# A decoder step's input product: seven products for eight in four more quads, another order of groups, recurrence tables per pair

## The chip, the core and the metric

The kernel runs on one core of a Trainium2 chip. The metric is the device time of one execution in microseconds (us); less is better.

## The reference

One layer of a hybrid decoder over 2048 prompt tokens and 64 sample tokens (8 sequences of 8), 2112 in all, in float32. The parts that matter here:

```python
xn = rms_norm(x, norm_pre)                               # (tokens, 1024)
z = jnp.einsum('btd,de->bte', xn, w_in)                  # w_in 1024 x 4096
v_pool, g_pool, u_lru, g_lru = ...                       # four times 1024 columns of z
y_pool, new_pool = pool_mixer(v_pool, pool_buf, ...)     # sliding means of 2, 4, 8, 16 tokens
                                                         # by channel group, then a 256x256 map
xs, new_conv = causal_conv(u_lru, conv_buf, ...)         # width 4, per channel
y_lru, new_h = rg_lru(xs, h0, ...)                       # two gates by 128x128 matmuls per head,
                                                         # then h = a*h + u along the tokens
mixed = jnp.concatenate([y_pool * silu(g_pool), y_lru * silu(g_lru)], -1)
out = jnp.einsum('bte,ed->btd', mixed, w_out)            # w_out 2048 x 1024
return x + rms_norm(out, norm_post), new_pool, new_conv, new_h
```

The pool and LRU mixers carry state along the tokens, so the tokens go through in order.

## The kernel before

**Tiling.** The tokens are cut into three thirds m = 0, 1, 2 of 704 (two column halves of 352 each, `CW`). In each third the product with `w_in` is done in 16 *quads* (m, p, kind): the kind is V (pool input), G (pool gate), U (LRU input) or L (LRU gate), and p = 0..3 is a group of 256 channels. A quad is a 2 x 2 block problem: two halves of the 1024 inputs, two blocks of 128 channels, two halves of the tokens. Names carry all three: `wG2_...` is a weight tile of G of group 2 in the first third, `w1G2_5` the one for product 5 of the same quad in the second.

**Products.** Every float32 operand is split into a high part (ACT casts it to fp32r, `x_hi` and `hi_lo`) and the rest (DVE subtracts, `x_lo`); a product adds hi·hi, hi·lo and lo·hi, so one product of 512 inputs is 4 x 3 = 12 matmuls of 128 x 352 (`quad_product`). In the first third a quad takes 8 plain products (`plain_slot`). In the second and third thirds it takes 7 products of sums of blocks, in the manner of Strassen and Winograd (`quad_slot`), numbered 1, 5, 6, 3, 2, 7, 4. They build up in three PSUM tiles: `a` takes 1, 6, 7, 4 in turn, `e` takes 5, 3, and `d` takes 2; after each, ACT copies the tile out (`put_copy`) or DVE adds it to what was copied (`put_sum`), and PE may not write the tile again before that. The x operands X11, T1, T2, X22, T3, X21, T4 are blocks of x and sums of blocks, in an SBUF tile XN; the `transition` between two thirds makes them. The weight operands are sums of blocks of `w_in`, made on DVE from four raw tiles (`s_sums`), split, used, and stored to a DRAM tile `wsd` from which later thirds load them. A quad of the second third that finds no stored sums and makes its own from raw tiles is a *late* quad (`is_late`). For V and G of groups 1, 2 and 3 the sums are made during the first third, with nothing to use them there (`s_early`), so ten of the second third's 16 quads are late.

**After the product.** V quads feed the pool chain (scan, differences, a map by 128 x 128 matmuls, names `y`, `dh`, `dl`, `pw`), U quads the convolution and the gate matmuls (`r`, `i`, `xh`, `xl`, `lw`), L and G quads SiLU gates. The LRU recurrence runs per head in `lru_chain`: tanh, square root, arctan and two sines on ACT, which need three sets of ACT tables, then a scan on DVE. Results go to DRAM (`mixed`). Last comes the product with `w_out`.

**What sets the order.** A planner in the kernel's own code writes the program out. `one_slot` issues one product, then `run_jobs` lets waiting jobs (generators that ask for an engine, a wait or a DMA) fill ACT, DVE and GpSimd to the end of that slot by estimated costs; a job's rank adds a small penalty. Each engine then runs its instructions in exactly this order. Weight tiles turn over in `W_BUFS = 7` buffers and are asked for `AHEAD = 6` slots before use; raw tiles have eight buffers, two quads' worth. All loads of weights and x go out in order from the one queue of SP. In the first third groups come 0, 1, 2, 3, and so in the others.

```python
key = {1: "a", 6: "a", 7: "a", 4: "a", 5: "e", 3: "e", 2: "d"}[pid]
...
if not first:
    pe_after(t["f" + key])      # not before the tile's last copy or sum
...
W_BUFS = 7
```

At the second transition the first blocks of `w_out` (`wb11_0` to `wb11_4`) are loaded and cast too (`region_chain`), into the space of the tile XA that held the raw x.

Of the kernel before, what the change touches and what calls it, by code (L numbers as in the profile page):

```python
# [16 lines left out]
P = 128  # L17
# [43 lines left out]
AHEAD = 6  # L61
TABLE_COST = 1.4
# [5 lines left out]
X_LEAD = (5, 5)  # L68
# [7 lines left out]
def hymba_kernel(  # L76
# [24 lines left out]
    def t_done(n):  # L101
        t_live[0] -= n
# [107 lines left out]
    XA = sb.tile([P, 4 * QW], F32, tag="XA", bufs=1, name="XA")  # L210
# [18 lines left out]
    def q_raw(name):  # L229
        if name in "AB":  # L230
            i = "AB".index(name)
            return XA[:, 2 * QW * i:2 * QW * (i + 1)]
        return XN[:, BASE[name]:BASE[name] + 2 * QW].bitcast(F32)
# [3 lines left out]

    def q3(name, i):
        b = BASE[name] + i * QW
        return XN[:, b:b + QW].rearrange("p (k t) -> p k t", t=CW)  # L240

    def xq(name, k, i):
        b = BASE[name] + i * QW + k * CW
        return XN[:, b:b + CW]
# [126 lines left out]
    def region(r, k, i):  # L371
        p = (r * KT + k) * 2 + i
        if p >= 10:
            p -= 10
            return XN[:, PIECE * p:PIECE * (p + 1)]
        if not x2_box:
            x2_box.append(sb.tile([P, 4 * QW], F32R, tag="XA", bufs=1, name="XA2"))
        return x2_box[0][:, PIECE * p:PIECE * (p + 1)]
# [83 lines left out]
    def product_short(bank, a, r):  # L462
        for k in range(KT):
            ah = a[k // 4][:, (k % 4) * P:(k % 4 + 1) * P]
# [45 lines left out]
    def short_a(q):  # L510
# [3 lines left out]
        for e in range(2):  # L514
            t = t_tile(f"as{q}_{e}", F32R)[:, :PIECE] if e else x2_box[0][:, 10 * PIECE:11 * PIECE]
            ts.append(t)
# [3 lines left out]
            h3 = t.rearrange("p (b t) -> p b t", t=P)  # L520
            split(h3[:, :, :n], h3[:, :, n:2 * n], r, nc.scalar, nc.vector)
# [200 lines left out]
    for m_ in range(NM):  # L722
        for p_ in range(NG):
            L_ = [(m_, p_ - 1, "L")] if p_ else []
            if m_ == LM and p_ == NG - 1:
                QUADS += [(m_, p_, "V")] + L_ + [(m_, p_, "U"), (m_, p_, "G")]
            elif (m_, p_) == (0, 1):
                QUADS += L_ + [(m_, p_, "V"), (m_, p_, "G"), (m_, p_, "U")]
            else:
                QUADS += [(m_, p_, "V"), (m_, p_, "G")] + L_ + [(m_, p_, "U")]  # L730
        QUADS.append((m_, NG - 1, "L"))
# [19 lines left out]
    def spawn(gen, ready=None, rank=2, then=()):  # L751
        job = {"gen": gen, "ready": T[0] if ready is None else ready, "rank": rank, "then": list(then)}
# [30 lines left out]
    def run_jobs(end):  # L783
        moved = True
        while moved:
# [14 lines left out]
            for job in jobs:  # L800
# [3 lines left out]
                req = job["req"]  # L804
                late = s + (TABLE_COST if len(req) > 2 and table[0] not in TABLES[req[2]] else 0.0)
                late += PENALTY[job["rank"]]
# [20 lines left out]
    IDLE = [XN[:, BASE[n] + 1024 * i:BASE[n] + 1024 * (i + 1)] for n in ("X11", "T2", "T1") for i in range(2)]  # L827
    S_OF = {5: "22", 6: "11", 7: "21", 3: "12"}
    n_idle = [0]
# [35 lines left out]
    def plain_tile(q, n):  # L865
        t = w_tiles[q, n] = half_tile(f"w{q[2]}{q[1]}_{n}")
        store = (flat_of(t), q[2], q[1], PLAIN_PID[n]) if n in PLAIN_PID else None
        w_jobs[q, n] = spawn(hi_lo(t[:, 0, :], t[:, 1, :], w_rawt[q, n], store, (q, n)), rank=0)
# [20 lines left out]
    def s_early(q):  # L889
        def made(i):  # L890
            n = n_idle[0] % len(IDLE)
            b = IDLE[n]
            n_idle[0] += 1
            if n in places:
                force(places[n], True)
            places[n] = spawn(hi_lo(b[:, :512], b[:, 512:], w_rawt[q, S_OF[S_PID[i]]], (b, q[2], q[1], S_PID[i])),
                              clock["V"] + HOP, rank=1)
            early.append(places[n])
        early.append(spawn(s_sums(q, made), rank=1))

    early, places = [], {}
# [1062 lines left out]
```

## Time and profile before

| | before |
|---|---|
| median of 3 runs | 1156.71 us (1156.38 to 1162.74) |
| profiled execution | 1159.3 us |
| its span, first to last instruction | 1157.6 us |
| mean granted TensorE clock | 0.995 |
| PE busy | 1127.9 us (97%) |
| DVE busy | 826.7 us (71%) |
| ACT busy | 656.0 us (57%), 88.5 of it in 69 table loads |
| GpSimd (POOL) busy | 160.4 us (14%) |
| DMA | 322.10 MB, mean 278 GB/s |

PE is TensorE's matmuls, DVE is VectorE, ACT is ScalarE, SP the engine that issues most DMAs. Names such as L323 are lines of the kernel. In waits, "A <- B" says that A's engine stood idle until B's was done. A granted clock under 1.00 means that PE ran slower than full speed. The second third's first product starts at 296 us, the third third's at 551, the output product at 815.

### The profile page before, as it was taken

The page shows a single profiled execution, that of the slowest core. Times are in us where ns is not written, and L with a number is a line of the kernel's source. Part 1 is how long each engine was busy: PE and PEld are TensorE (multiplying, and loading weights), DVE is VectorE, ACT ScalarE, POOL GpSimd, SP SyncE. Part 2 cuts the span into 40 slices and gives each one's busy share as a digit, 9 for nine tenths or more (in the row PEclk, how much of TensorE's full clock was granted, in tenths as well). Part 3 has the DMA queues.
Part 4 walks back from the last instruction along what each step waited for, and adds up shares of the span by engine and source line. Part 5 has one row for each costly group of instructions (what it writes and reads, how often), then busy time and mean ns, then how long its engine had stood idle before and what let it go on. Part 6 is the DMA issues. An engine that isn't in the chain of part 4 may idle for free. (4 is left out here: it accounts for less than half of the span.)

```text
span 1157.6 us, 17742 instructions
## 1 busy us (share of the span) xinstructions
PE 1127.9 (97%) x6274; PEld 1056.3 (91%) x6274; DVE 826.7 (71%) x1323; ACT 656.0 (57%) x1112; POOL 160.4 (14%) x264
## 2 busy tenths in 40 slices
PE   7999999999999999999899999999999999999996
PEld 6999999999999999989899999999888888888885
DVE  6796783859768667578857674746567678778777
ACT  5376658777577847567464846374755233344232
POOL 4200100002001010101111111101000003211232
PEclk9999999999999999999999999999999999999999
DMA  9656877895897889996989999998679677776563
GB/s 329 233 195 234 306 279 272 325 352 185 292 342 271 317 319 326 382 387 225 370 280 380 397 351 370 358 353 292 207 202 291 182 207 221 207 233 185 164 182 127
DMA packets 177464, 322.10 MB, mean 278 GB/s; under 512 B 24736, under 2 KB 86432, under 8 KB 177376
## 3 DMA queue, kind: packets, MB, share of 16 engines
q1 hardware_dynamic: 173536, 303.67, 76.3%
q0 software_dynamic: 3840, 17.30, 3.8%
q8 instruction: 49, 0.80, 0.3%
q14 instruction: 39, 0.32, 0.1%
HBM read 218.51 MB, written 102.15 MB: 277 GB/s over the span
## 5 line engine op out<-in xcount | busy, mean ns | idle before, releaser
L151 ACT ACT_TABLE_LOAD x69 | 88.5, 1283 | 1.9 <-PEq L1943 0.8
L458 PE MATMUL p<-XN,s 128*128 128x512 f32 (+1 forms) x224 | 86.8, 387 | 0.0
L459 PE MATMUL p<-XN,s 128*128 128x512 f32 (+1 forms) x224 | 86.8, 387 | 0.0
L460 PE MATMUL p<-XN,s 128*128 128x512 f32 (+1 forms) x224 | 86.7, 387 | 0.0
L1217 DVE SCALAR_TENSOR_TENSOR xs<-u,parT,xs 128x704 f32<-128x704 f32 (+1 forms) x72 | 67.8, 956 | 16.1 <-ACT xs L1206 15.9
L451 POOL TENSOR_TENSOR xr<-ac,xr 128x512 f32<-128x512 f32 x27 | 48.5, 1815 | 207.1 <-DVE ac L592 97.7
L1180 DVE SCALAR_TENSOR_TENSOR g<-y,parT,g 128x352 f32<-128x352 f32 x48 | 27.9, 582 | 53.9 <-PE y L253 53.2
L253 PE MATMUL zL<-XN,wL 128*128 128x352 f32 x384 | 65.0, 325 | 0.6 <-DVE wL L323 0.6
L253 PEld LDWEIGHTS zL<-XN,wL 128*128 128x128 f32 x384 | 62.7, 188 | 0.9 <-DVE wL L323 0.9
L140 ACT CAST s<-a 128x512 fp32r<-128x512 f32 x48 | 28.7, 616 | 57.8 <-DVE a L451 44.9
L571 ACT ACTIVATE p<-ac 128x512 f32<-128x512 f32 (+1 forms) x32 | 18.8, 587 | 75.1 <-DVE ac L451 75.1
L451 DVE TENSOR_TENSOR a<-a,a 128x512 f32<-128x512 f32 x48 | 33.0, 690 | 29.7 <-DMA a<-mixed 25.6
L458 PE MATMUL p<-XN,a 128*128 128x512 f32 x137 | 54.2, 396 | 0.0
L460 PE MATMUL p<-XN,a 128*128 128x512 f32 x137 | 54.2, 396 | 0.0
L459 PE MATMUL p<-XN,a 128*128 128x512 f32 x137 | 54.2, 395 | 0.0
L253 PE MATMUL y<-dh,pw 128*128 128x352 f32 x192 | 54.1, 323 | 0.0
L460 PEld LDWEIGHTS p<-XN,s 128*128 128x128 f32 x224 | 42.1, 188 | 9.5
L459 PEld LDWEIGHTS p<-XN,s 128*128 128x128 f32 x224 | 42.1, 188 | 9.5
L458 PEld LDWEIGHTS p<-XN,s 128*128 128x128 f32 x224 | 42.1, 188 | 9.4
L253 PE MATMUL zV<-XN,wV 128*128 128x352 f32 x288 | 48.6, 324 | 0.0
L253 PE MATMUL zU<-XN,wU 128*128 128x352 f32 x288 | 48.2, 324 | 0.0
L253 PE MATMUL zG<-XN,wG 128*128 128x352 f32 x288 | 47.9, 325 | 0.0
(343 smaller groups left out, 3093.9 us busy)
## 6 DMA issues: line engine op xcount, KB each, us to landing
a<-mixed SPq DMA_DIRECT2D x112, 256.0 KB, 4.2
mixed<-g POOLq DMA_DIRECT2D x48, 352.0 KB, 6.0
w2V<-wsd SPq DMA_DIRECT2D x28, 512.0 KB, 7.1
w2G<-wsd SPq DMA_DIRECT2D x28, 512.0 KB, 7.2
w2U<-wsd SPq DMA_DIRECT2D x28, 512.0 KB, 7.5
w2L<-wsd SPq DMA_DIRECT2D x28, 512.0 KB, 7.6
wsd<-XN SPq DMA_DIRECT2D x27, 512.0 KB, 6.4
w1V<-wsd SPq DMA_DIRECT2D x24, 512.0 KB, 6.7
```

The costliest lines, as they stand in the source:

```text
L140: hi_eng.copy(out=hi, in_=src)
L151: nc.scalar.preload_act_table_set(name)
L253: nc.tensor.matmul(out, lhsT=lhsT, rhs=rhs, start=start, stop=stop)
L451: (eng or nc.vector).tensor_tensor(out=out, in0=a, in1=b, op=op)
L458: nc.tensor.matmul(out, lhsT=ah, rhs=wh, start=start and k == 0, stop=False)
L459: nc.tensor.matmul(out, lhsT=ah, rhs=wl, start=False, stop=False)
L460: nc.tensor.matmul(out, lhsT=al, rhs=wh, start=False, stop=stop and k == KT - 1)
L571: nc.scalar.activation(out=junk, in_=o, func=AF.Square, accum_out=st[:, g:g + 1])
L1180: V.scalar_tensor_tensor(out=g[:, cs], in0=Y, scalar=col(C_SCALE, blk), in1=g[:, cs], op0=ALU.mult, op1=ALU.mult)
L1217: V.scalar_tensor_tensor(out=xs, in0=E[:, k:k + n], scalar=col(C_CW + 8 * k, b), in1=xs, op0=ALU.mult, op1=ALU.add)
```

## The change

1. *Four quads by seven products.* V and G of groups 2 and 3 in the first third (`is_made`) go through `quad_slot`, in the order 1, 5, 6, 3, 7, 2, 4 (`ORDER_0`). Their x operands (`XOF_0`) are the three blocks that already stand in XN as plain operands (X22, T3, T4) and four sums that `first_sums` makes in the first third, from three quads ahead (`X0_LEAD`), in the slots X11, T1, T2 and in a new tile XT4 in the space of XA's first half. `made_sums` and `made_tile` make the weight sums, which are also stored for the second third. `s_early` is gone, so V and G of group 1 are late: 12 late quads instead of 10.
2. *Order of groups.* `P_ORDER`: 0, 1, 2, 3 in the first third, 2, 1, 3, 0 in the second, 1, 2, 3, 0 in the third.
3. *Recurrence per pair.* `lru_chain` is split into `lru_gate`, `lru_pair` and `lru_chain`; `lru_pair` does tanh, square root and the three trigonometric steps for the two heads of a quad together, so 47 table loads stand in the program instead of 70.
4. *Raw weights* of a quad are asked for up to `RAW_AHEAD = 14` slots ahead of its first product, and jobs have due times: a job whose time is near has no penalty, another has the largest (`behind`).
5. *x of the next third.* `X_LEAD` goes from 5 and 5 quads to 7 and 10. XA becomes two tiles, XAA and XAB; the second half is loaded first, and the first half of the second third's x waits until the made quads have used XT4 (`x0_free`). The sums T1, T2, T4 of a transition are formed in the tiles of x itself.

```diff
+RAW_AHEAD = 14
+PACE = 2.1
+URGENT = 2.0
+X0_LEAD = 3
+FROM_P = 2
+P_ORDER = ((0, 1, 2, 3), (2, 1, 3, 0), (1, 2, 3, 0))
-X_LEAD = (5, 5)
+X_LEAD = (7, 10)
+XOF_0 = {1: "X22", 5: "X11", 6: "T2", 3: "T4", 7: "T1", 2: "T3", 4: "A"}
+ORDER_0 = (1, 5, 6, 3, 7, 2, 4)
...
+    def is_made(q):
+        return q[0] == 0 and q[1] >= FROM_P and q[2] in EARLY
+
     def is_late(q):
-        return q[0] == 1 and (q[1] == 0 or q[2] not in EARLY)
+        return q[0] == 1 and (q[1] < FROM_P or q[2] not in EARLY)
...
+    def behind(job, s, req):
+        due = job["due"]() if job["due"] else None
+        if due is None:
+            b = PENALTY[job["rank"]]
+        else:
+            slack = (due - now[0]) * PACE - (s - T[0]) - (2.2 if req[0] == "A" else 1.5)
+            b = 0.0 if slack < URGENT else PENALTY[-1]
...
-    def s_early(q):
...
+    MADE_SUMS = ((5, None), (6, 1), (7, 5), (3, 6))
+    made = {}
+
+    def made_sums(q):
+        r11, r12, r21, r22 = (w_rawt[q, n] for n in NAMES)
+        for pid, split_of in MADE_SUMS:
+            yield "?", lambda: split_of is None or (q, split_of) in w_fin
+            yield "V", 0.68
+            if pid == 5:
+                tadd(r21, r21, r22)
+            elif pid == 6:
+                tsub(r11, r21, r11)
+            elif pid == 7:
+                tsub(r21, r22, r11)
+            else:
+                tsub(r11, r12, r11)
...
-        need_x(XOF[pid], q[0])
-        quad_product(z, w, XOF[pid], first, True, True)
+        x_name = XOF[pid] if q[0] else XOF_0[pid]
...
+        quad_product(z, w, x_name, first, True, True)
...
+    def lru_pair(q, heads):
+        m, p, _ = q
+        for j in range(2):
+            b, r = 2 * p + j, heads[j]["r"]
+            yield "A", 0.98, "tanh"
+            act_table("tanh")
+            AC.activation(out=r, in_=r, func=AF.Tanh, scale=lam2[:, b:b + 1], bias=lam2[:, b:b + 1])
+        for j in range(2):
+            r = heads[j]["r"]
+            yield "A", 0.8, "sqrt"
+            act_table("sqrt")
+            AC.activation(out=r, in_=r, func=AF.Sqrt)
+        for j in range(2):
...
+            AC.activation(out=r, in_=r, func=AF.Arctan)
+            AC.activation(out=v, in_=r, func=AF.Sin, scale=2.0)
+            AC.activation(out=u, in_=r, func=AF.Sin, scale=-2.0, bias=half_pi)
+            spawn(lru_chain(q, j, heads[j]), clock["A"] + HOP, rank=1)
...
+            if m == 1 and h == 0:
+                yield "?", lambda: x0_free
+                x_tiles["A"] = xa_tile("A", "XA1")
...
+    def first_sums():
+        X = x_quarter
...
+            yield "A", 1.37
+            x_hi(n, src)
+            yield "V", 1.65
+            x_lo(n, src, V)
+            x0_fin[n] = clock["V"] + HOP
+        for n, out, a, b in (("X11", X(0, 0), X(0, 1), X(0, 0)), ("T1", X(0, 1), X(1, 1), X(0, 1)),
+                             ("T2", X(1, 1), X(1, 1), X(0, 0)), ("A", X(1, 0), X(1, 0), X(1, 1))):
             yield "V", 1.75
...
+                if first_of[QUADS.index(q)] - n > RAW_AHEAD:
+                    break
```

Over the whole program TensorE has 48 matmuls of 128 x 352 less (4656 instead of 4704), DVE 22 instructions more, ACT 21 fewer; the output product is unchanged.

**TensorE in V of group 2, first third.** The first plain product stands just ahead of these rows; `y` is a matmul of the pool map of another group, `zV2_...` the PSUM tiles, `wV2_11` to `wV2_22` the four plain blocks of the weight. Before:

```order
L253 MATMUL y0111_1487<-dh0_11_1267,pw0_1_1226 128x352
L253 MATMUL zV2_0_1473<-XN_95,wV2_12_1407 128x352 x12
L253 MATMUL zV2_2_1527<-XN_95,wV2_21_1433 128x352 x12
L253 MATMUL zV2_2_1527<-XN_95,wV2_22_1454 128x352 x12
L253 MATMUL zV2_4_1561<-XN_95,wV2_11_1386 128x352 x12
L253 MATMUL zV2_4_1561<-XN_95,wV2_12_1407 128x352 x12
L253 MATMUL zV2_6_1599<-XN_95,wV2_21_1433 128x352 x12
L253 MATMUL zV2_6_1599<-XN_95,wV2_22_1454 128x352 x12
```

Now, from the second product on (`XT4_...` is the new x sum):

```order
L267 MATMUL e0V2_1492<-XN_96,wV2_5_1359 128x352 x12
L269 MATMUL y0111_1506<-dh0_10_1233,pw0_1_1215 128x352
L269 MATMUL y0111_1506<-dl0_10_1250,pw0_1_1215 128x352
L269 MATMUL y0111_1506<-dh0_10_1233,pw0_1_1215 128x352
L269 MATMUL y0111_1506<-dh0_11_1253,pw0_1_1215 128x352
L269 MATMUL y0111_1506<-dl0_11_1269,pw0_1_1215 128x352
L269 MATMUL y0111_1506<-dh0_11_1253,pw0_1_1215 128x352
L267 MATMUL a0V2_1468<-XN_96,wV2_6_1387 128x352 x12
L267 MATMUL e0V2_1492<-XN_96,wV2_3_1409 128x352 x12
L267 MATMUL a0V2_1468<-XN_96,wV2_7_1430 128x352 x12
L267 MATMUL d0V2_1583<-XN_96,wV2_2_1454 128x352 x12
L267 MATMUL a0V2_1468<-XT4_1059,wV2_4_1483 128x352 x12
```

Eight products in four tiles have become seven in three; `a0V2` is written by 1, 6, 7, 4 with one product between most of them.

**SP around the raw tiles of an L quad, second third.** `wr1L2` are the four raw tiles of L of group 2 (of `in_w_in`), `w1G3_...` the stored sums of G of group 3, which comes just ahead of it in the order of quads. Before:

```order
L907 DMA w1G3_2_5054<-wsd_92 128x1024
L907 DMA w1G3_7_5073<-wsd_92 128x1024
L352 DMA wr1L2_11_5080<-in_w_in 128x512
L352 DMA wr1L2_12_5082<-in_w_in 128x512
L352 DMA wr1L2_21_5084<-in_w_in 128x512
L352 DMA wr1L2_22_5086<-in_w_in 128x512
L907 DMA w1L2_1_5102<-wsd_92 128x1024
L1329 DMA XA_94<-in_xt 128x2x704
L907 DMA w1G3_4_5157<-wsd_92 128x1024
```

Now the like place, at the raw tiles of L of group 1, which also follows G of group 3:

```order
L984 DMA w1V3_2_4232<-wsd_92 128x1024
L368 DMA wr1L1_11_4253<-in_w_in 128x512
L368 DMA wr1L1_12_4255<-in_w_in 128x512
L368 DMA wr1L1_21_4257<-in_w_in 128x512
L368 DMA wr1L1_22_4259<-in_w_in 128x512
L984 DMA w1V3_7_4261<-wsd_92 128x1024
L984 DMA w1G3_1_4277<-wsd_92 128x1024
L984 DMA w1G3_5_4292<-wsd_92 128x1024
L984 DMA w1V3_4_4307<-wsd_92 128x1024
L1029 DMA lw1_1_4309<-swd_93 128x1024
L984 DMA w1G3_6_4328<-wsd_92 128x1024
L984 DMA w1G3_3_4348<-wsd_92 128x1024
```

The raw tiles went out behind six of G3's seven weight tiles and next to the first weight tile of their own quad; now they go out ahead of all of G3's.

**ACT at the second transition.** `wb11_0` is the first block of `w_out`, `e2G0`, `e2G1` and `a2G1`, `a2V1` PSUM tiles of quads of the third third. Before:

```order
L1085 ACTIVATE g31_1_5601<-g31_1_5601 128x704
L1025 COPY g8_2_5892<-a2G0_5896 128x352
L1463 CAST XA2_5937<-wb11_0_5913 128x512
L1025 COPY g9_2_5893<-e2G0_5917 128x352
L1025 COPY e1_2_5754<-a2V0_5757 128x352
L1222 CAST xh6_1_5979<-xs6_1_5691 128x704
L1025 COPY g8_2_5892<-a2G0_5896 128x352
```

Now:

```order
L1105 COPY g10_2_5896<-a2G1_5900 128x352
L1587 CAST X2A_5942<-wb11_0_5917 128x512
L1105 COPY g11_2_5897<-e2G1_5923 128x352
L1587 CAST X2A_5942<-wb11_1_5939 128x512
L1587 CAST X2A_5942<-wb11_2_5969 128x512
L1105 COPY e3_2_5739<-a2V1_5742 128x352
L1332 ACTIVATE rg1_1_5989<-r11_0_5958,hb_102 128x352
L1332 ACTIVATE rg1_1_5989<-r11_1_5959,hb_102 128x352
L1105 COPY g10_2_5896<-a2G1_5900 128x352
```

The cast still stands directly ahead of the copy of an `e2G` tile; two more casts follow it ahead of the copy of `a2V1`.

More of the change, by code (lines that the diff above doesn't have):

```diff
@@ L803, in run_jobs @@
                     continue
[L804 to L806 removed]
+                late = s + behind(job, s, job["req"])
                 if best is None or late < best[0] - 0.05:
@@ L887, in s_sums @@
             made(i)
-    def s_early(q):
[L890 to L901, printed above, removed]
+    MADE_OF = {1: "11", 5: "21", 6: "11", 7: "21", 3: "11", 2: "12", 4: "22"}
@@ new lines, in made_need @@
+    def made_need(q, pid):
+        if (q, pid) in w_fin:
+            return
+        box = made[q]
+        while pid in S_OF and pid not in box["sums"]:
+            split_of = MADE_SUMS[len(box["sums"])][1]
+            if split_of:
+                made_need(q, split_of)
+            job = box["job"]
+            if job["req"][0] == "?":
+                advance(job)
+            grant(job, max(clock["V"], job["ready"], T[0]))
+        job = w_jobs[q, pid]
+        while (q, pid) not in w_fin:
+            if job["req"][0] in clock:
+                grant(job, max(clock[job["req"][0]], job["ready"], T[0]))
+            else:
+                advance(job)
@@ new lines, in need_x0 @@
+    def need_x0(n):
+        if n in XOF_0.values() and n not in x0_fin and n in ("X11", "T1", "T2", "A"):
+            job = x0_jobs["sums"]
+            while n not in x0_jobs:
+                grant(job, max(clock["V"], job["ready"], T[0]))
+            if n == "A":
+                for o in ("X11", "T1"):
+                    need_x0(o)
+            job = x0_jobs[n]
+            while n not in x0_fin:
+                if job["req"][0] == "?":
+                    advance(job)
+                grant(job, max(clock[job["req"][0]], job["ready"], T[0]))
+        pe_after(x0_fin.get(n, 0.0))
```

293 lines of the change are left out of this document (172 added, 121 removed).

## The prediction

> **What bounds the kernel.** I read the busy shares first, then the table by stretches, then the waits of TensorE.
>
> ```profile
> span 1157.6 us, 17742 instructions
> PE 1127.9 (97%) x6274; PEld 1056.3 (91%) x6274; DVE 826.7 (71%) x1323; ACT 656.0 (57%) x1112; POOL 160.4 (14%) x264
> ```
>
> TensorE (PE) is busy for 97% of the span; no other engine passes 71%. The time is therefore PE's work plus its gaps, and an edit counts only where it takes matmuls out or opens or closes a gap. In the table by stretches the columns are the stretch, its length, busy time and instructions of PE, weight loads, DVE, ACT and POOL, then granted PE clock, DMA share and GB/s.
>
> ```profile
> 137.00:243.00 106.00, 106.00 (x655) 106.00 (x654) 76.53 (x119) 77.30 (x130) 8.73 (x26) 1.00 0.84 310
> 460.00:480.00 20.00, 20.00 (x125) 20.00 (x124) 11.57 (x16) 12.75 (x21) 4.35 (x11) 1.00 1.02 417
> 480.00:500.00 20.00, 19.93 (x124) 19.65 (x123) 9.79 (x14) 9.87 (x21) 1.16 (x3) 1.00 1.03 359
> 500.00:520.00 20.00, 17.33 (x99) 16.85 (x99) 16.24 (x29) 13.56 (x27) 0.00 (x0) 0.91 1.00 380
> 600.00:800.00 200.00, 197.19 (x1202) 194.90 (x1201) 131.09 (x207) 116.52 (x179) 28.22 (x71) 1.00 0.98 361
> ```
>
> The first row is the part of the first third in which the four pool quads of groups 2 and 3 lie: PE has no gap at all, and one matmul takes 106.00/655 = 0.162 us, a product of 12 matmuls 1.94 us. At 500 PE loses work and clock. The waits (total, times, longest) say to whom:
>
> ```profile
> PE e2G L251 <- ACT g L1025: 3.6, 2, 3.1
> PE a1G L251 <- DVE g L1021: 2.7, 1, 2.7
> PE e2V L251 <- DVE XN L323: 1.7, 1, 1.7
> PE a2L L251 <- DMA w2L<-wsd: 0.8, 2, 0.5
> ```
>
> Three single waits, at 504, 553 and 575, are most of what PE loses in the second and third thirds.
>
> **The change part by part.**
>
> *Seven products for eight.* Four quads lose one product each: 4 x 12 = 48 matmuls. PE is full there, so each is worth its 0.162 us: **-7.8 us**. What is added stands on other engines:
>
> ```profile
> L323 DVE TENSOR_TENSOR XA<-XA 128x704 f32<-128x704 f32 x12 | 10.1, 886 | 0.1
> L323 DVE TENSOR_TENSOR XN<-XA,XN 128x1408 fp32r<-128x1408 f32 x16 | 25.7, 1620 | 4.9 <-ACT XN L338 4.9
> L338 ACT CAST XN<-XA 128x1408 fp32r<-128x1408 f32 x16 | 21.9, 1372 | 12.3 <-DVE XA L1666 11.2 <-PE d1L L251 0.6 <-PE zL L253 0.2
> L323 DVE TENSOR_TENSOR wr1L<-wr1L,wr1L 128x512 f32<-128x512 f32 x12 | 8.3, 689 | 0.2
> 505.99 0.52 DVE L1021 TENSOR_TENSOR g<-a1G,g 128x352 f32<-128x352 f32 x1
> ```
>
> Four x sums: on DVE 8 x 0.886 + 4 x 1.62 = 13.6 us, on ACT 4 x 1.37 = 5.5 us. Twelve more sums out of PSUM: 12 x 0.52 = 6.2 us of DVE. The weight sums of these four quads are made and stored in the first third, as before; those of group 1 move into the second third: 8 sums and 8 splits of 0.69 = 11.0 us of DVE leave the one and enter the other, and four splits go for good (2.8 us). The first third thus gets about 13.6 + 6.2 - 11.0 - 2.8 = 6 us more of DVE. In the first row above DVE idles for 29.5 us of 106; beside PE this costs nothing. Were that cover gone, it would cost its 6 us.
>
> *Evacuations.* In a plain quad two products lie between one use of a PSUM tile and the next. In the new order 1, 5, 6, 3, 7, 2, 4 the tile a is used by 1, 6, 7, 4 and e by 5, 3, with one product (1.94 us) between most uses: 4 gates in each of 4 quads, 16 in all. I price them by the nearest rows: the later thirds have 32 quads with about 4 such gates each, and the rows above show three evacuation waits there, 3.6 + 2.7 = 6.3 us over 128 gates, 0.05 us a gate; 16 gates make 0.8. With 0.7 for a DMA wait or two more of the size of the a2L row, **+1.5 us**. The ends are 0 (the gates of the second third other than one show no wait) and 28 (the second rival).
>
> *Raw weights 14 slots ahead.* This goes for the wait at 504.
>
> ```profile
> 482.57 5.16 SPq L352 DMA_DIRECT2D wr1L<-in_w_in  x4
> 495.09 0.69 DVE L326 TENSOR_TENSOR wr1L<-wr1L,wr1L 128x512 f32<-128x512 f32 x1 [8.79 <-DMA wr1L<-in_w_in]
> 497.88 2.10 PE L251 MATMUL a1G<-XN,w1G 128*128 128x352 f32 x12
> 501.78 2.11 PE L251 MATMUL e1L<-XN,w1L 128*128 128x352 f32 x12
> 506.56 3.68 PE L251 MATMUL a1G<-XN,w1G 128*128 128x352 f32 x12 [2.67 <-DVE g L1021]
> ```
>
> The raw tiles went out at 482.57 and held DVE until 495.09, 12.5 us. DVE, in order, then had its backlog ahead of the sum that frees a1G, which started at 505.99 though the product had ended at 499.98. PE lost 2.67 us idle and 3.68 - 2.12 = 1.56 of slow clock. In the changed order seven or more products stand between the raw loads of an L quad and its first sum, two quads ahead, 12 to 25 us of PE against 6 to 11. I take the wait as gone: **-4.2 us**; the other end is 0, should the same latency hit another quad.
>
> *Transitions.* The wait at 553 is that for the lower half of an x sum:
>
> ```profile
> 553.00 0.32 PE L251 MATMUL e2V<-XN,w2V 128*128 128x352 f32 x1
> 555.04 2.05 PE L251 MATMUL e2V<-XN,w2V 128*128 128x352 f32 x11 [1.71 <-DVE XN L323]
> ```
>
> The x work now starts up to ten quads ahead, and the sum for this product is done one quad earlier. But T3's lower half now stands on DVE behind a PSUM sum and two raw sums of T4: 0.52 + 2 x 0.886 + 1.62 = 3.9 us, while from the product that releases the PSUM sum to the one that reads T3 PE has a product and six short gate matmuls, 1.94 + 6 x 0.162 = 2.9. So 1.7 us go and 1.0 comes: **-0.7 us**, between -1.7 and +0.5.
>
> Then the wait at 575, for ACT:
>
> ```profile
> 567.29 0.43 SPq L391 DMA_DIRECT2D wb<-in_w_out  x1
> 576.84 0.62 ACT L1463 CAST XA<-wb 128x512 fp32r<-128x512 f32 x1 [7.50 <-DMA wb<-in_w_out]
> 577.37 0.45 ACT L1025 COPY g<-e2G 128x352 f32<-128x352 f32 x1
> 577.86 3.37 PE L251 MATMUL e2G<-XN,w2G 128*128 128x352 f32 x12 [3.14 <-ACT g L1025]
> 581.03 2.52 PE L251 MATMUL d2G<-XN,w2G 128*128 128x352 f32 x12
> ```
>
> A block of w_out sets out at 567.29 and its cast waits until 576.84, 9.5 us, ahead of the copy that frees e2G. The price was 3.14 idle and (3.37 - 2.12) + (2.52 - 2.12) = 1.65 of slow clock, 4.8 us. The same cast stands ahead of the same copy in the changed order; only 54 matmuls (8.7 us) instead of 48 (7.8) lie between the product that lets the DMA go and the one that needs the copy, and the transfers due around it are 8.9 MB in 31.0 us of PE (287 GB/s) instead of 9.4 in 28.2 (333). With the same latency the wait is 3.14 - 0.9 = 2.2, less the slow clock, so 2 to 2.6 of the 4.8 go; with the median latency all of it:
>
> ```profile
> wb<-in_w_out SPq DMA_DIRECT2D x24, 256.0 KB, 3.6
> ```
>
> Three casts now stand there, not one, so I do not take the whole: **-2.8 us**, between 0 and -4.8.
>
> A rule of the Trainium skill bears on the slow clock: "TensorE: Matmul & The Clock Gate", "Why this matters for your kernels", asks for no PE gap over about 3 us. Here a gap of 2.67 us already brought the clock to 0.91 and one of 1.71 did not; by the page the first would have cost its 2.67 alone, and the sum would be -12.5.
>
> *Tables per pair.* ACT drops 23 of its table loads:
>
> ```profile
> L151 ACT ACT_TABLE_LOAD x69 | 88.5, 1283 | 1.9 <-PEq L1943 0.8
> 530.63 1.28 ACT L151 ACT_TABLE_LOAD   x1
> 531.92 0.79 ACT L1269 ACTIVATE rg<-rg 128x704 f32<-128x704 f32 x1
> 532.75 0.79 ACT L1270 ACTIVATE xs<-rg 128x704 f32<-128x704 f32 x1
> 533.45 0.87 ACT L1271 ACTIVATE w<-rg,half_pi 128x704 f32<-128x704 f32 x1
> ```
>
> 23 x 1.283 = 29.5 us of ACT, all beside a busy PE and an ACT at 57%: 0.
>
> *What is only moved.* Another group order puts the same products in another sequence; its price is the density of transfers, the first rival. The A half of x for the second third now waits on SP for the last made product (G of group 3). Behind it on SP stand three stores and, some four products on, the raw tiles of L of group 3, which are used some 30 us of PE later; x itself has 27 products (52 us) until V of group 2 needs it: 0, and at most one product's 1.94 if the wait reached a loaded weight. The halved tiles of x and of the short rows and the output product behind them issue the same matmuls: 0.
>
> Sum: -7.8 + 1.5 - 4.2 - 0.7 - 2.8 = **-14.0 us**. The profiled execution took 1159.3 us (span 1157.6), so it would be 1145.3; it lies 2.6 above the median of the runs, 1156.71, and on that the forecast is **1143 us**.
>
> **The rivals.**
>
> *First: DMA in the second third.* With two more late quads and raw loads drawn forward, three quads in a row (L of group 2, U of 1, V of 3) now issue 6.3 + 7.2 + 6.7 = 20.2 MB (counted from the transfers in the order, 128 x columns x 4 bytes) in 44.7 us of PE, 452 GB/s; the densest three before had 411. At the 417 GB/s of 460 to 480, 20.2 MB take 48.4 us: 3.7 late and, at a clock of 0.91 for a while, about 5: 1148. At the 361 GB/s of 600 to 800 they take 56.0: 11 late, 1154. For it: queues at share 1.0 for 60 us. Against it: weights go out six slots ahead, and in the 417 row PE was full. "DMA: Bandwidth & Descriptors" of the Trainium skill, "Specifications", gives 358 GB/s per core from HBM; by it the delay would be 11.7 us. The trace moved 417 for 20 us, so here the page's figure is no ceiling.
>
> *Second: the new gates become the bound.* If ACT stands in a table load and the arctan and sine steps (1.28 + 0.79 + 0.79 + 0.87 = 3.7 us) when a product ends, the copy is 3.7 - 1.94 = 1.8 late; at all 16 gates 28 us, and 1143 + 28 - 1.5 = **1169**, slower than before. It decides from the point where ACT or DVE reach the tile more than 1.94 us after the product at nearly every gate. Against it: ACT's and DVE's load in the first row, 73% and 72%, and a copy placed behind each product in the order. A quarter of it gives 1148.
>
> *Third: only the matmuls count.* Late loads hit other quads and the three gaps come back elsewhere: -7.8 alone, **1149**.
>
> *Fourth: all gaps close*: -7.8 - 4.2 - 1.7 - 4.8 = -18.5, 1138.
>
> **How the numbers follow.** Forecast 0.62, first rival 0.12, second 0.07, third 0.11, fourth 0.08. Within 1% of 1156.7 (about what a measurement of this kernel can tell from no change) is 1145.1 to 1168.3. Of the forecast I put 0.54 below 1145.1 and 0.08 above, since D alone (the wait at 575) can shift it by 2.8; the first rival adds 0.02 to faster and 0.10 to same, the third 0.11 to same, the fourth 0.08 to faster. Faster 0.64, same 0.29, slower 0.07. The range 1136 to 1154 holds the forecast with its unknown terms, the third and fourth rivals and the first up to 361 GB/s; the second is left out.
>
> **What would show it.** Right: 48 fewer matmuls with PE at no gap from 137 to 235; no a1G wait on DVE in the second third; an e2G wait on ACT of about 2 us. Wrong: waits of a0V, a0G, e0V or e0G on ACT or DVE; w1 waits on DMA around 365 to 410; a wait for T3's lower half above 1 us. The forecast fails if the gaps were not caused by these places but by whatever is late when the queues are full, for then they move and do not go.

## The result, and the profile after

The changed kernel takes **1150.51 us** (median of 11 runs, 1147.37 to 1154.47) against 1156.71 before (11 runs, 1154.11 to 1162.74). The ratio is 0.9938, 95% interval 0.9916 to 0.996: a gain of 0.6%, about 6 us of the 14 forecast. The profiled execution took 1153.73 us (before 1159.3), at a granted clock of 0.993 (before 0.995); the two lie 3.2 and 2.6 us above the medians of their kernels. The page of the changed kernel begins with these rows:

```profile
span 1152.0 us, 17682 instructions
PE 1119.7 (97%) x6226; PEld 1048.8 (91%) x6226; DVE 842.2 (73%) x1345; ACT 629.4 (55%) x1091; POOL 162.3 (14%) x264
L160 ACT ACT_TABLE_LOAD x46 | 59.0, 1283 | 1.5 <-PEq L2092 0.8
```

The 48 matmuls are gone (6274 to 6226) and so are 23 table loads. PE's busy time fell by 8.2 us, which is all of the 7.8 for the matmuls; the rest of the forecast, the gaps, is what failed to come on balance. Where it went shows when both traces are cut at the first product of each stage:

| stage, us | before | after | difference | forecast |
|---|---|---|---|---|
| to the first product of the second third | 296.1 | 293.3 | -2.8 | -6.3 |
| second third | 255.0 | 254.2 | -0.8 | -4.2 |
| third third | 264.4 | 258.5 | -5.9 | -3.5 |
| output product and rest, to the end of the span | 342.1 | 346.0 | +3.9 | 0 |

12 gate matmuls (1.95 us) moved from the second third into the first, so the first row is 36 matmuls lighter and the second 12. The waits of TensorE in the changed kernel (in all, times, longest), those of the first microseconds left out:

```profile
PE p L477 <- DVE s L152: 2.1, 1, 2.1
PE r L269 <- DMA lw<-swd: 2.0, 2, 1.3
PE a1V L267 <- DMA w1V<-wsd: 1.8, 1, 1.8
...
PE a2L L267 <- DMA w2L<-wsd: 1.7, 1, 1.7
PE e1V L267 <- DMA w1V<-wsd: 1.6, 1, 1.6
PE r L269 <- ACT xh L1306: 1.0, 1, 1.0
PE a2V L267 <- DVE XN L339: 0.9, 1, 0.9
```

None of the three single waits of before stands here with its old size: a1G on DVE and e2G on ACT are gone, and 0.9 of a2V is what is left of e2V's 1.7. All the others shown are new or larger. Four places matter.

*The made quads* cost PE nothing, as the table by stretches shows (length, busy time and instructions of PE, weight loads, DVE, ACT, POOL, clock, DMA share, GB/s):

```profile
137.00:243.00 106.00, 106.00 (x656) 106.00 (x655) 83.28 (x127) 74.50 (x126) 10.27 (x23) 1.00 0.83 302
400.00:410.00 10.00, 8.53 (x53) 8.24 (x51) 0.53 (x1) 3.06 (x6) 1.19 (x5) 1.00 1.03 407
410.00:420.00 10.00, 8.14 (x38) 7.64 (x39) 4.54 (x7) 3.34 (x6) 0.78 (x1) 0.83 0.99 361
```

DVE went from 76.53 to 83.28 us there, 6.7 more (forecast 6), and PE has no gap.

*Queues full at 400 to 420*, second and third rows: PE, which was full there before, loses 3.3 us idle, and more by the clock of 0.83. The time line (start, duration, then engine, line, operation) names the loads:

```profile
410.08 2.18 PE L267 MATMUL e1V<-XN,w1V 128*128 128x352 f32 x12 [1.55 <-DMA w1V<-wsd]
...
416.23 3.68 PE L267 MATMUL a1V<-XN,w1V 128*128 128x352 f32 x12 [1.78 <-DMA w1V<-wsd]
```

With 3.68 - 2.12 of slow clock that is 1.55 + 1.78 + 1.56 = 4.9 us, more than the 4.2 that went at 504.

*The start.* At 80 us PE waits for ACT and then runs at half clock:

```profile
80.82 0.43 PE L269 MATMUL r<-xh,lw 128*128 128x352 f32 x1 [1.02 <-ACT xh L1306]
81.94 0.66 PE L269 MATMUL r<-xl,lw 128*128 128x352 f32 x1 [0.69 <-DVE xl L339]
...
83.57 2.91 PE L269 MATMUL zV<-XN,wV 128*128 128x352 f32 x12
```

ACT is late because its cast of `pw` waits longer for a DMA; here are the cast and SP's issues, of before first:

```profile
73.97 0.62 ACT L957 CAST pw<-pwr 128x512 fp32r<-128x512 f32 x1 [2.61 <-DMA pwr<-in_pool_w]
...
70.68 0.42 SPq L938 DMA_DIRECT2D pwr<-in_pool_w  x1
79.95 1.89 SPq L352 DMA_DIRECT2D wr0G<-in_w_in  x4
```

and of the changed kernel:

```profile
76.19 0.62 ACT L1037 CAST pw<-pwr 128x512 fp32r<-128x512 f32 x1 [4.52 <-DMA pwr<-in_pool_w]
...
64.16 2.13 SPq L368 DMA_DIRECT2D wr0G<-in_w_in  x4
...
70.99 1.64 SPq L1018 DMA_DIRECT2D pwr<-in_pool_w  x1
```

The four raw tiles of G now go out 16 us earlier, ahead of `pwr`. That is itself issued only 0.3 us later, but its cast comes 2.2 us later. Of the two gaps on PE only the first is new: the kernel before has the one of 0.69 at the same product too.

*The output product* has the same matmuls as before but takes 3.9 us more, with the longest wait of the whole list near its end, for a split `s` on DVE:

```profile
1121.50 0.50 PE L477 MATMUL p<-XN,s 128*128 128x512 f32 x1 [2.14 <-DVE s L152]
```

SP issues the load `s2r` that this split needs at 1112.78, just behind a store of a finished row:

```profile
1109.85 0.35 SPq L617 DMA_DIRECT2D out<-xr  x1
...
1111.56 0.34 SPq L617 DMA_DIRECT2D out<-xr  x1
1112.04 0.33 SPq L588 DMA_DIRECT2D xr<-in_x  x1
1112.78 0.32 SPq L647 DMA_DIRECT2D s2r<-s2d  x1
```

The chain of work that ended last passes through this place (start, duration, what): GpSimd's last add to a row, the row's store, the reload of `xr`, the load `s2r`, a step of DVE, and from there DVE and ACT in turn to the end.

```profile
1108.14 1.69 POOL xr L468
...
1109.85 2.12 DMA out<-xr
...
1112.04 0.33 SPq L588
...
1112.78 1.83 DMA s2r<-s2d
...
1116.57 0.69 DVE s2r L468
```

The chain of the kernel before has the same link, but there this last `s2r` goes out 302.4 us after the first output product, and here 306.7.

### The profile page after: what moved, and what is told of

It is laid out like the page before. It is cut to its first block, busy times and chain, and to the rows that moved or that the text cites. A ratio compares the mean times of both kernels' runs of the same rounds, so it can differ in the third digit from the quotient of the medians.

```text
span 1152.0 us, 17682 instructions
## 1 busy us (share of the span) xinstructions
PE 1119.7 (97%) x6226; PEld 1048.8 (91%) x6226; DVE 842.2 (73%) x1345; ACT 629.4 (55%) x1091; POOL 162.3 (14%) x264
## 5 line engine op out<-in xcount | busy, mean ns | idle before, releaser
L1273 POOL DMA_DIRECT2D mixed<-g x24 | 13.2, 549 | 296.1 <-ACT g L1105 59.7
L269 PEld LDWEIGHTS zU<-XN,wU 128*128 128x128 f32 x288 | 46.9, 188 | 0.0
```

The source lines that it names most:

```text
L269: nc.tensor.matmul(out, lhsT=lhsT, rhs=rhs, start=start, stop=stop)
L1273: nc.gpsimd.dma_start(out=mixed[:, blk, m * MW:(m + 1) * MW], in_=g[:, :MW])
```

## The experiments

All edits are to the changed kernel, except one that is to the kernel before. Ratios are to the kernel before, with 95% intervals. Where a stage is named, its length is that of the one profiled execution, cut as in the table above. Such a length moves by some 2 us between executions of the same instructions: up to the second third, experiments 2, 7 and 10 run the changed kernel's own program, and took 293.6, 291.4 and 293.0 us against its 293.3.

**1. The 48 matmuls put back.** Are they worth their full time, or does a chain in the output product set the end?

```diff
+        if is_made(q) and pid == 2:
+            quad_product(z, w, x_name, True, True, True)
```

Product 2 is done twice in the four made quads.

> The changed kernel with the last but one product of each of the four made quads run twice (the second run overwrites the first with the same value): 48 matmuls of 128x352 are put back where the change took them out, nothing else differs. Theory one (the output product at the end is held by its own chain of loads and VectorE sums, which arrive only about 5.5 us earlier than before although TensorE arrives 10 us earlier): of the 7.8 us that 48 matmuls take, about 4 are seen, 1150.5 to 1154.5, and the 2.1 us wait at the first sum operand near 1121 us with its slow clock is gone. Rival (TensorE's work sets the end all the way): the full 7.8 us, 1158.

Measured: 1158.1 us (1153.93 to 1164.97, 10 runs), ratio 1.001 (0.999 to 1.003), 7.6 above the changed kernel. The matmuls are worth their 7.8 us. The first third grew by 7.1, the output product kept 345.6, and the wait near its end stayed, 1.70 instead of 2.14, though all came 6 us later:

```profile
1127.73 0.50 PE L477 MATMUL p<-XN,s 128*128 128x512 f32 x1 [1.70 <-DVE s L152]
```

So that wait is no fixed end against which PE runs: it moves with PE, and the extra 4 us are lost within the output product itself.

**2. x of the next third later.**

```diff
-X_LEAD = (7, 10)
+X_LEAD = (7, 8)
```

> The changed kernel with the loads of x for the last third begun 8 quads before the end of the second third instead of 10: the three densest quads of the second third then issue 409 GB/s instead of 452. Theory one (the two waits of a1V and e1V for weights at 410 to 416 us, 3.3 us and 1.6 us of slow clock, come from this density): both waits go, and the kernel gains 3 to 5 us at that place; how much of it is left at the end depends on the output product, so 1146 to 1150. Rival (these waits are a matter of one late transfer that any order has somewhere): a wait of like size for stored weights stands elsewhere in the second third and the time stays at 1150.5.

Measured: 1149.9 us (5 runs), ratio 0.9945 (0.9925 to 0.9965). The waits for w1V at 410 are gone, and the second third took 252.3 instead of 254.2; two other waits came:

```profile
469.45 0.72 PE L267 MATMUL a1U<-XN,w1U 128*128 128x352 f32 x3 [2.08 <-DVE tok L316]
506.40 2.61 PE L267 MATMUL a1L<-XN,w1L 128*128 128x352 f32 x12 [1.22 <-ACT w1L L890]
```

So the x loads that were drawn forward by two quads stood behind the waits at 410; but by its time alone this edit can't be told from no change.

**3. Raw weights 8 slots ahead, everywhere, and 4. in the first 16 slots only.**

```diff
-RAW_AHEAD = 14
+RAW_AHEAD = 8
```

```diff
-                if first_of[QUADS.index(q)] - n > RAW_AHEAD:
+                if first_of[QUADS.index(q)] - n > (8 if n < 16 else RAW_AHEAD):
```

> The changed kernel with raw weights asked for at most 8 slots ahead instead of 14, everywhere. Theory one: the new wait of the first gate product at 80 us (1.0 us for the cast of the convolution, with 1.3 to 1.6 us of slow clock) comes from the raw tiles of the second G quad, which now go out ahead of the load of the pool map's weights; it goes, 2 to 3 us at that place. In the second third the free raw buffers, not the 14 slots, decide when raw tiles go out, so the wait of a1G that the kernel before had at 504 us does not come back. Rival (the 14 slots are what removed that wait): a wait on VectorE of 2 to 4 us comes back in a G or L quad of the second third and the time is 1150 to 1153.

> The changed kernel with 8 slots in place of 14 in the first 16 slots alone (the first quads of the first third). Theory one: only the wait at 80 us with its slow clock goes, 2 to 3 us there; all else as in the changed kernel. Together with the run that has 8 slots everywhere it tells the two places apart: if both have the same time, the 14 slots do nothing in the second third. Rival (the wait at 80 us is not due to this order of loads): the wait stays and the time is 1150.5.

Measured: 1148.01 us (ratio 0.993, 0.9905 to 0.9955) and 1148.47 us (0.9933, 0.9917 to 0.995), four runs each. Against the changed kernel's 0.9938 (0.9916 to 0.996) neither can be told apart by time alone; the traces tell. Stage one took 290.7 and 290.4 us instead of 293.3, and the cast is back at its old place, here in the third experiment:

```profile
73.72 0.62 ACT L1037 CAST pw<-pwr 128x512 fp32r<-128x512 f32 x1 [2.61 <-DMA pwr<-in_pool_w]
```

The four profiles with the changed kernel's own program up to there (its own and those of experiments 2, 7 and 10) give 292.8 us on average, the four with 8 slots there (these two and experiments 11 and 12) 290.9, from 290.4 to 291.5. So the 14 slots cost about 1.9 us at the start, and up to 3 in an execution in which a slow clock follows the gap.

With 8 slots no a1G wait comes back either. The raw tiles of the L quad near 500 still go out well ahead there, at 476.27 for a first sum at 491.66; 14 slots instead of 8 buy nothing in the second third that these runs show. With 8 slots everywhere the waits for w1V shrink as well, from 3.3 us to the 0.9 of one e1V.

**5. Recurrence tables per head again**, with the new planner kept:

```diff
-                if len(heads) == 2:
-                    spawn(lru_pair(q, heads), clock["A"] + HOP, rank=1)
+                spawn(lru_pair(q, {j: heads[j]}), clock["A"] + HOP, rank=1)
...
-        for j in range(2):
+        for j in sorted(heads):
```

> The changed kernel with the ACT steps of the recurrence per head again, as soon as a head's gates are done (63 table loads in the program instead of 47). Theory one (tables per pair lie beside a busy TensorE and are worth nothing, as the prediction had it): 1149 to 1152, and the w1V waits near 410 us and the wait near 1121 us stay. Rival a (the loads are on the path): 16 x 1.28 = 20 us of ACT come back and some of it shows, 1154 to 1160. Rival b (the pair delays the recurrence, so that VectorE enters the output product behind; from there VectorE trails TensorE by 14 to 18 matmuls more than in the kernel before, up to the wait of 1 to 2.5 us near 1115 to 1121 us): the trailing shrinks, that wait goes and the time falls to 1146.

Measured: 1156.3 us (10 runs), ratio 0.9987 (0.9966 to 1.0009), 5.8 above the changed kernel (the two profiled executions are 2.6 apart). There are 63 table loads instead of 47. The third third took 268.4 us instead of 258.5; 12 matmuls that come after the first output product in the changed kernel are in it (1.95 us). The waits of that third here:

```profile
PE a2V L267 <- DVE XN L339: 3.5, 3, 1.9
PE e2G L267 <- DMA w2G<-wsd: 1.8, 2, 1.4
PE a2L L267 <- DMA w2L<-wsd: 1.6, 2, 1.5
```

Few of them name ACT: the 16 more loads are not seen to stop PE there themselves, but the planner's clock puts everything else in other places. Which of these is the cause was not separated.

The output product went the other way, as rival b had it: it took 339.5 us, 341.5 with those 12 matmuls counted in, about the 342.1 of the kernel before, and PE has no wait near its end. So what the change loses there comes back when the tables are loaded per head again, while the third third loses more than that.

**6. Groups in the order 0, 1, 2, 3 in all thirds.**

```diff
-P_ORDER = ((0, 1, 2, 3), (2, 1, 3, 0), (1, 2, 3, 0))
+P_ORDER = ((0, 1, 2, 3), (0, 1, 2, 3), (0, 1, 2, 3))
```

> The changed kernel with the groups in the order 0, 1, 2, 3 in all three thirds; the four late quads V and G of groups 0 and 1 then all stand at the head of the second third. Theory one (the order only sets where transfers are dense: the three densest quads have 432 GB/s instead of 452): the w1V waits at 410 us go or shrink, others of 1 to 3 us appear around L of group 0, and the time is 1148 to 1153. Rival (the order is what removed the wait of a1G at 504 us): a wait of 2 to 4 us on VectorE comes back near a quad G with an L quad's raw tiles behind it, 1153 to 1157.

Measured: 1154.48 us (10 runs), ratio 0.9976 (0.9959 to 0.9992), 4.0 above the changed kernel. The a1G wait does not come back, so the new order is not needed to keep it away; instead a load is late in the third third:

```profile
614.98 2.69 PE L267 MATMUL e2G<-XN,w2G 128*128 128x352 f32 x12 [3.58 <-DMA w2G<-wsd]
```

This execution took 1151.98 us, less than the changed kernel's profiled one, so it does not show where the 4.0 between the medians is lost; and the two intervals just touch.

**7. Splits of the output product one step further ahead, in its last 12 steps.**

```diff
-        while n_prep < len(preps) and n_prep - i < 3:
+        while n_prep < len(preps) and n_prep - i < (4 if i >= len(order) - 12 else 3):
```

> The changed kernel with the operands of the last 12 products of the output made four products ahead instead of three. From the profiles: the last 80 us of VectorE take the same 80.2 to 80.7 us in the kernel before and in the changed ones, whatever TensorE's lead. Theory one (VectorE's operands wait there for loads that stand on SP behind the stores of finished rows): the loads go out earlier, the wait of p for s near 1121 us (2.1 us and its slow clock of 1.7) goes, 1146 to 1148. Rival (VectorE's own work or GpSimd's additions set these 80 us): the wait stays and so does the time, 1150.5.

Measured: 1151.58 us (7 runs), ratio 0.9933 (0.991 to 0.9957): no change. The stage took 346.3 us. PE's waits in it fell from 2.14 us to 1.2, in two parts, yet from PE's last matmul to the end it took 11.9 us instead of 9.5. So PE's wait near 1121 does not set the end; the chain of loads and DVE steps behind it does. Preparing earlier does not help, which leaves the data's arrival.

**8. Two made quads instead of four** (groups 3 only), for a dose.

```diff
-FROM_P = 2
+FROM_P = 3
```

The made quads now come so late that the x of the second third is loaded over that of the first while its sums are still being made; part of the sums are of the wrong x.

> The changed kernel with seven products in V and G of group 3 alone: V and G of group 2 take eight again, and 24 matmuls come back; these two quads are late too, 14 late quads, and in the second third one quad, V of group 3, has 608 GB/s of transfers. Theory one (each product is worth its 1.95 us and the rest is where the transfers are dense): 3.9 us back and the w1V waits at 410 us at least as long, 1154 to 1157. Rival (making the quads by seven products costs what it saves, in copies and sums at the 16 gates): 8 gates less, 1148 to 1151.

Measured: 1176.12 us (4 runs), ratio 1.0158 (1.0123 to 1.0194). The experiment failed: in the second third PE waits 15 us, for x sums of the transition and for w1 loads, so two things changed at once, and the question of the dose stays unanswered.

**9. Recurrence per pair alone, on the kernel before**: `lru_chain` there split into `lru_gate`, `lru_pair` and `lru_chain`, with the old penalties and no due times.

```diff
-                spawn(lru_chain(q, j, rg[0], rg[1], xs), clock["A"] + HOP, rank=1)
+                heads = Q[q].setdefault("heads", {})
+                heads[j] = {"r": rg[0], "gi": rg[1], "v": xs}
+                spawn(lru_gate(heads[j]), clock["A"] + HOP, rank=1)
+                if len(heads) == 2:
+                    spawn(lru_pair(q, heads), clock["A"] + HOP, rank=1)
```

> The kernel before with one part of the change alone: the recurrence's ACT steps for both heads of a quad together (54 table loads in the program instead of 70); eight products, order, x and raw loads as before. Undone in the changed kernel, this part cost 5.8 us, against nothing in the prediction. Theory one (fewer loads leave ACT free for the copies and casts that TensorE waits for): a gain here too, 2 to 6 us, 1151 to 1155. Rival (in the run that undid it, only the order of all other work fell out worse by chance): 1156 to 1158 here.

Measured: 1182.58 us (4 runs), ratio 1.021 (1.0175 to 1.0245): 25 us slower, which no theory had. ACT's time line there:

```profile
433.37 1.28 ACT L151 ACT_TABLE_LOAD   x1
...
439.91 0.43 ACT L1025 COPY g<-a1G 128x352 f32<-128x352 f32 x1
```

and PE's at the same place:

```profile
426.19 2.10 PE L251 MATMUL a1G<-XN,w1G 128*128 128x352 f32 x12
...
440.39 3.89 PE L251 MATMUL a1G<-XN,w1G 128*128 128x352 f32 x12 [10.16 <-ACT g L1025]
```

The product ended at 428.3 and its copy starts at 439.91, behind the recurrence of two heads with its table loads, gate steps and casts between. A second such gap, 6.07 us, stands at 651. This is the mechanism of the second rival, at another place: with fewer tables, but a longer block of ACT ahead of a copy. In the changed kernel no recurrence stands on ACT at this time, and the copy starts at 428.78, 0.1 us after its product's end (426.58 + 2.12).

So the pairing pays in the changed kernel and not in the kernel before; whether the due times are what keeps such a block from standing ahead of a copy was not tried alone.

**10. Stores of finished rows on GpSimd's queue.**

```diff
-            nc.sync.dma_start(out=y[lo:hi, h * PIECE:(h + 1) * PIECE], in_=xs[h])
+            nc.gpsimd.dma_start(out=y[lo:hi, h * PIECE:(h + 1) * PIECE], in_=xs[h])
```

> The changed kernel with the stores of the finished output rows issued by GpSimd, which makes their last sum, and no longer by SP, where loads stand behind them (SP waits 49.7 us for GpSimd in the output product). The output product and what follows take 342.1 us in the kernel before and 344.7 to 346.3 in every kernel with tables per pair and 1456 matmuls there. Theory one (this section is held by loads that stand behind those stores): it falls by 2 to 4 us, the wait near 1121 us goes, 1146 to 1149. Rival (VectorE's and GpSimd's own work holds it, as the run with operands made one product earlier suggests): no change, 1149 to 1152.

Measured: 1145.63 us (4 runs), ratio 0.9892 (0.9863 to 0.992). The output stage took 339.9 us instead of 346.0, and PE has no wait left in it. What SP's queue waits for from 800 to 1150 us, in the changed kernel first:

```profile
SPq L617 <- POOL xr L468: 49.7, 25, 6.1
```

and in this experiment:

```profile
SPq L588 <- DMA out<-xr: 56.7, 22, 9.7
```

SP waits no less than before, but elsewhere: not at the store, with the loads behind it, but at the reload of `xr` once the splits' loads are out. Its issues near the end show it:

```profile
1101.00 1.25 SPq L647 DMA_DIRECT2D s2r<-s2d  x2
1103.28 27.78 SPq L588 DMA_DIRECT2D xr<-in_x  x7
```

The last `s2r` load goes out about 298 us after the first output product instead of 306.7, and the chain that ended last now runs through PE's matmuls. The store of a finished row waits for GpSimd's add; moved out of the loads' queue it holds up none of the splits' loads.

**11. Experiments 2 and 3 together, and 12. these with 10.**

> The changed kernel with both of the edits that took a wait away: raw weights 8 slots ahead and x of the last third from 8 quads before. Theory one (each wait has its own cause, so the gains add): 1146 to 1148, and neither the wait at 80 us nor the w1V waits near 410 us show. Rival (a wait that goes is replaced by another, since the transfers of the second third fill the queues whatever their order): 1148 to 1150, with one or two waits of 1 to 2 us elsewhere in the second third.

> The changed kernel with the three edits that helped: raw weights 8 slots ahead, x of the last third from 8 quads before, and the stores of the output rows issued by GpSimd. Theory one (the start, the second third and the output product lose time separately, so the gains add): 1144.3 less the 4.9 us of the stores, 1138 to 1141, and the output product with what follows about 340 us. Rival (the output product is held by VectorE's own 80 us at its end, and a TensorE that comes earlier waits there): 1143 to 1145, with the section at 343 to 344 us.

Measured: 1144.3 us (4 runs), ratio 0.9879 (0.9849 to 0.9909), and **1139.61 us** (1139.39 to 1139.96, 4 runs), ratio 0.9848 (0.9822 to 0.9874). The last beats both kernels, the one before by 17 us and the changed one by 11. Together the two loads' edits bring more than apart: the second third takes 249.7 us, and PE is full where it waited at 410 (experiment 11, by stretches):

```profile
400.00:410.00 10.00, 10.00 (x64) 10.00 (x62) 3.51 (x5) 3.44 (x6) 0.79 (x1) 1.00 1.02 414
410.00:420.00 10.00, 10.00 (x63) 10.00 (x63) 4.92 (x7) 4.36 (x8) 1.70 (x3) 1.00 1.03 406
```

The queues are as full as before, at share 1.02 and the same GB/s: only what stands in them first is another, so a full queue alone does not make PE wait. Of the two waits that experiment 2 had brought, that of a1U did not arise with both; a1L's 1.2 us stayed.

## Why the prediction was right and wrong

The time lies in the range, 7.5 us above the forecast, near the first rival's 1148 and the third's 1149, and within the 1% that had been given 0.29. That it lies there is in part luck: the gaps that the sum counted on did close, and others opened that it held at nothing or gave to a rival, 2.8, 4.9 and 3.9 us in the profiled execution. By its steps:

- **Seven products for eight, -7.8: right.** Experiment 1 gives 7.6 by the medians, and the cover held: 6.7 us more of DVE beside a full PE.
- **Evacuations, +1.5: too dear.** Not one of the 16 gates shows a wait, so their 0.8 was 0; the second rival did not happen here. (With 8 raw slots a few do: a0V waits for ACT 0.4, 0.3 and 1.1 us in experiments 3, 11 and 12.) Experiment 9 shows that its price, when ACT's blocks do stand ahead of a copy, is real.
- **Raw weights, -4.2: right, as far as shown.** The a1G wait went. At the L quad near 500 the raw tiles now go out 17.4 us ahead of their first sum, within the 12 to 25 foreseen, DVE no longer waits for them, and it reaches the sum that frees a1G as the product ends:

```profile
477.32 2.00 SPq L368 DMA_DIRECT2D wr1L<-in_w_in  x4
494.71 0.68 DVE L342 TENSOR_TENSOR wr1L<-wr1L,wr1L 128x512 f32<-128x512 f32 x1
499.85 0.53 DVE L1101 TENSOR_TENSOR g<-a1G,g 128x352 f32<-128x352 f32 x1 [0.37 <-PE a1G L267]
```

  It needs neither 14 slots (experiment 3) nor the new order of groups (experiment 6). But no run put the raw loads back to where the kernel before had them, and the due times weren't undone, so which of the two removed the wait is not isolated.
- **The same edit at the start: the step that failed first.** The forecast looked at the 14 slots only where they cure a wait. SP issues in order in the first third as well, where `wr0G` now stands ahead of `pwr`; that cost about 2.8 us in the profiled execution (a new gap of 1.02 and the slow clock behind it), and 1.9 by the means of the profiles with 14 and with 8 slots.
- **Transitions: right, and better.** The lower half was to be 1.0 us late:

```profile
562.45 2.05 PE L267 MATMUL a2V<-XN,w2V 128*128 128x352 f32 x11 [0.91 <-DVE XN L339]
...
573.09 2.12 PE L267 MATMUL e2G<-XN,w2G 128*128 128x352 f32 x12
```

  It is 0.91 late. The e2G products, at 566.28 and 573.09, run at 2.12 without a wait, so the whole 4.8 at 575 went, not 2.8. The third third gained 5.9, of which these two are 5.6.
- **Tables per pair, 0: wrong.** Undone they cost 5.8, alone they cost 25. That ACT's time beside a busy PE is free leaves out what the planner makes of it, in the order of the other instructions: pairing gains in the third third, and loses in the output product (experiment 5).
- **What is only moved, 0: probably wrong for the order of groups.** Undone it costs 4.0 by the medians, with intervals that touch; one wait of 3.58 for a load is seen, but the place of the loss is not shown.
- **First rival: it came, beside the forecast's gains**, at the place named (w1 loads, 365 to 410), in V of group 3, the last of its three quads: 4.9 us, as worked out from 417 GB/s (about 5). That the sizes agree so well is luck in part, since 1.6 of it is slow clock, which experiment 1 with gaps of the same size did not have. It had been given 0.12 as an alternative to the sum; it was a term of it. The trace moved 407 GB/s at 400 to 410, so the 358 of the Trainium skill ("DMA: Bandwidth & Descriptors", "Specifications") is no ceiling here either, and its 11.7 us did not come.
- **The output product, 0: the largest loss that no rival named.** "The same matmuls" held, and the same time did not: +3.9. Its loads share SP's queue with stores that wait for GpSimd, and experiment 10 takes the loss away, and some more. Of the parts that were undone, the tables per pair are the one that brings it back to the time of the kernel before (341.5, experiment 5). By which step they make the same order of loads later is open; one of GpSimd's adds before the split runs slowly (below), but that was not tried by itself.

With the sizes that the two profiled executions give, the sum is -7.8 + 2.8 (start) - 4.2 + 4.9 (second third) - 0.8 - 4.8 (third) + 3.9 (output) = -6.0; the spans differ by 5.6.

## What to carry to other kernels

A load that is drawn forward in an in-order queue is paid for by every load behind it, in every stage in which the rule applies; look at what stands behind it, not only at the wait that it is to cure. A store that waits for a slow engine does not belong in the queue that feeds the bottleneck: moved to another it was worth 5 us. And a rival that acts at another place than the forecast is a term of the sum, not an alternative to it.

## What the runs showed that was not expected

The slow clock needs no long gap, and the same gap does not always bring it. In the changed kernel the gaps at 80 us (1.02 and 0.69) and at 416 (1.78), shown above, were each followed by 3.41 us of half clock: zV took 2.91 us and a1V 3.68, and the granted clock from 410 to 420 was 0.83. In experiment 1 PE's time line has the same gaps, longer ones even, and the products behind them at their usual length:

```profile
81.58 0.42 PE L269 MATMUL r<-xh,lw 128*128 128x352 f32 x1 [1.50 <-ACT xh L1308]
...
83.61 2.11 PE L269 MATMUL zV<-XN,wV 128*128 128x352 f32 x12
...
423.30 2.19 PE L267 MATMUL a1V<-XN,w1V 128*128 128x352 f32 x12 [1.84 <-DMA w1V<-wsd]
```

So a gap of 1 to 2 us costs itself, and at times some 1.6 us more; what decides is not shown. The Trainium skill ("TensorE: Matmul & The Clock Gate", "Why this matters for your kernels") asks for no gap over about 3 us; here less was enough at times.

The same two GpSimd adds (`xr`) in a row took 6.50 us in the changed kernel (at 1015.86) and 4.69 in experiment 5 (at 1021.72) and in the kernel before; what slows them was not tried. The changed kernel's 11 runs span 7 us, the 4 of experiment 12 only 0.6; whether its fewer waits are the reason is not shown.
